# One layer of a hybrid decoder on one core: two-pass broadcasts and gates, longer pauses, two-block attention, and half of the score scaling on GpSimd

## The chip, the cores and the metric

One Trainium2 chip, one of its cores. The time is device microseconds of one launch of the whole layer. A core has TensorE (matrix products; the profile calls it PE, its weight loads PEld), VectorE (DVE), ScalarE (ACT), GpSimd (POOL) and SyncE (SP, which here issues nearly all DMAs). The profile's clock column is the share of TensorE's full clock that was granted.

## What is computed

One layer of a decoder, 1024 tokens of 1024 channels, in float32. Three token mixers run on the same normalised input and are merged:

```python
u = rmsnorm(h, norm_mix)
(aq, ak, av, az, aa, ab,  bq, bk, bv, bo, bi, bf,
 cq, ckc, cvc, cks, cvs, ckw, cvw, cg, mg) = split_cols(u @ w_in, IN_SIZES)
y_a = gated_deltanet(aq, ak, av, az, aa, ab, ...)   # 4 heads of 128, chunks of 64
y_b = mlstm(bq, bk, bv, bo, bi, bf, ...)            # 4 heads of 128, chunks of 64
y_c = nsa(cq, ckc, cvc, cks, cvs, ckw, cvw, cg, ...)  # 8 query heads, 2 key groups, width 64
br = einsum("bsnc,ncd->bsnd", stack([y_a, y_b, y_c]), w_branch)
h = h + (sum over branches of sigmoid(mg) * br) @ w_out
h = h + (silu(u1 @ w_gate) * (u1 @ w_up)) @ w_ffn_out          # u1 = rmsnorm(h), inner width 2816
h = h + sigmoid(u2 @ w_ple_gate) * (p @ w_ple_proj)            # u2 = rmsnorm(h)
```

The DeltaNet mixer solves a unit triangular system for each chunk (here in blocks of 16, then two levels of products) and runs a scan over the chunks. The mLSTM mixer has exponential gates with a running maximum and a scan. The third mixer adds three attentions for each query: over 63 compressed blocks, over four selected blocks of 64 keys, and over a window of 512 keys; each has its own softmax and its own gate (`cg`), and the compressed scores choose the selected blocks.

## The kernel before

**Two-part products.** Most large products are made of float32 values split in two parts of a shorter type (float32r): `hi` is a rounded copy that ScalarE makes, `lo` the rest, `x - hi`, that VectorE or GpSimd makes. A product is then three products, hi x hi, hi x lo and lo x hi (`chan_block`, `tok_block`). Each weight block is 128 x 2048 and comes as four DMAs into `wraw`; `halve` (L429, L431) splits it into `whi` and `wlo` one block ahead, `load` fetches two blocks ahead. In the third stage VectorE makes every second `wlo`, in the others GpSimd makes all of them. A few products are in full float32; each of them shows as two records in the trace.

**Three stages.** The first runs the input projection as a list of blocks: the projection of `p`, the gates block, then for each DeltaNet head two blocks (q, k and v, z) and two or three blocks of merge gates for the first half of the tokens, then eight mLSTM blocks, five attention blocks and two more gate blocks. The second runs ten blocks of merge gates for the other half of the tokens, with attention beside them. The third runs the last two gate blocks, the six branch projections, the output projection, the FFN (its first pair of blocks as plain products, the ten others by a seven-product scheme on combined inputs, `utT1` to `utT4`), and the last gate.

**Sides.** Beside the blocks run generators ("sides") that issue the small work: gates, solves, scans, mLSTM heads and attention. A block yields between its groups of products, and `advance(n)` then lets the sides take n steps. At each of these `woven` grows by 1.4, the time of the block's products in that step. `pause(us)` stops a side until `woven` has grown by so much, so that products of blocks are issued to TensorE ahead of what follows; `behind()` ties the next products behind the block's last product. `later(lag, f)` calls f when the blocks' own product time has passed the lag. The rate is 2 steps in the first stage and 3.8 in attention. Each engine runs its queue in order; the order within the program is set at build time by a planner with its own costs, following the order in which the program was written where nothing stands against it. Named tiles come from pools: ten half tiles (`b2`), eleven and six whole tiles, eight banks of the product memory; a tile whose buffers are all in use waits for one.

**What the change touches.**

- `gates_block` (L609): 40 gate columns times `u`, one output tile, 2 halves x 8 x 3 products, then a scaled copy into `gaterows`; `gates_side` (L626) transposes that with eight small products (`gtr`) and derives all gates.
- `row_bcast` (L741): spreads a column over all rows. GpSimd multiplies the identity by the column (L747, `gcb_d`, `mrb_d`), and a full float32 product with a matrix of ones gives `gcb` (DeltaNet) or `mrb` (mLSTM). Two halves per head, four heads each.
- `gdn_solve` (L798): decay matrices, convolutions (L786), norms (`ktr`, L838), Gram matrices, the 16-wide triangular inverse on VectorE (`zb`, `xb`) with two trips through memory, a pause of 14, then the products `levq`, `levv`, `levw`, `levx`, `levy`. `levq` needs `gW` (L908).
- `nsa_keys` (L1243): splits and transposes keys (`khht`, `khtr`), with a pause of 3 before each half's transposes.
- `nsa_attend` (L1348): the list of attention tasks, window (w) or selected (s), query tile 0 to 7, pair of heads hp 0 or 1. Each turn issues the scores of one task in four steps and, in between, the values of the task before. `att_query` (L1377) loads, scales, splits and transposes a query tile (`qstk`, `qtr`) when its first scores begin. `att_scores` (L1400): the products `S`, the sum with the bias and the maximum on VectorE (L1453 to L1466), the exponential on ScalarE (L1472), then for each group and pair of heads on VectorE:

```python
nc.vector.tensor_tensor(sm[:, g], sm[:, g], gate[:, g], OP.mult)
for i in (n - 1, n):
    nc.vector.tensor_scalar(pts[i][:, :nk], pts[i][:, :nk], sm[:, g, i % 2:i % 2 + 1], None, OP.mult)
```

  (L1476, L1478). `att_values` (L1554): for each block of 128 keys four transposes (`ptr`) into one bank, a copy to `PT` by ScalarE or VectorE, and, one block behind, two value products (`nso`); at the end the compressed values, two products on quarters of the array (`nso<-PT,cv`).
- `load_y` (L1612): loads and splits a branch's output, all eight tiles at once.
- `ffn_combine` (L1754): sums of parts of `u`, whose low parts GpSimd makes (L1764). `put` (L1793) splits an activation, its low part (`alo`, L1796) on GpSimd.
- `ple_blocks`: the last addition (L1967) on GpSimd, then the store.

Of the kernel before, what the change touches and what calls it, by code (L numbers as in the profile page):

```python
# [38 lines left out]
COMBINE_LAG = 8.0  # L39
CMP_AT = 1, 3  # L40
# [19 lines left out]
def _constants():  # L60
# [44 lines left out]
    add("rowscale", np.where((m >= 4) & (m < 8), -1.0, 1.0))  # L105
# [30 lines left out]
def _blocks(w_in, w_branch, w_out, w_ffn_in, w_ffn_out, w_ple_gate, w_ple_proj):  # L136
# [7 lines left out]
    for dst, src, n in ((0, 2048, 4), (4, 4108, 4), (8, 2052, 4), (12, 4104, 4), (16, 5392, 24)):  # L144
        rows[:, dst:dst + n] = w_in[:, src:src + n]
# [81 lines left out]
class Trunk:  # L227
# [381 lines left out]
    def gates_block(self):  # L609
# [4 lines left out]
        def evac(ct, hf, ps):  # L614
            if hf == 0:
                self.tc.keep_in_program_order(
                    nc.vector.tensor_tensor(bias, self.chan["rowb"], self.rowscale, OP.mult))
            nc.scalar.activation(rows[:40, hf * 512:hf * 512 + 512], ps[:40], AF.Identity,
                                 bias=bias[:40], scale=self.rowscale[:40])
            if hf == 1:  # L620
                self.flags.add("rows")

        self.gaterows = rows
        return self.chan_block(self.u, evac, ncols=1)

    def gates_side(self):  # L626
# [3 lines left out]
        ps = self.ps("gtr")  # L630
        for tt in range(NT):
            self.tr(ps[:, tt * 40:tt * 40 + 40], self.gaterows[:40, tt * P:tt * P + P])
        gm = self.b2("gm")[:, :320].rearrange("p (t c) -> p t c", c=40)
        nc.scalar.activation(gm, ps[:, :320].rearrange("p (t c) -> p t c", c=40), AF.Copy)
# [39 lines left out]
        self.cum, self.gcol = cum, gcol  # L674
# [62 lines left out]
        self.ms, self.msc, self.msi, self.memt, self.mwks, self.mr = s, sc, si, emt, wks, r  # L737
# [3 lines left out]
    def row_bcast(self, col, name):  # L741
# [3 lines left out]
        for hf in range(2):  # L745
            d = self.b2(name + "_d")
            nc.gpsimd.tensor_tensor(d[:, :].rearrange("p (t c) -> p t c", c=P), bc(self.ident.unsqueeze(1), [P, 4, P]),  # L747
                                    bc(col[:, 4 * hf:4 * hf + 4].unsqueeze(2), [P, 4, P]), OP.mult)
            ps = self.ps(name)
            self.mm(ps, self.ones, d)  # L750
            out.append(ps)
# [46 lines left out]
    def gdn_solve(self, h):  # L798
# [10 lines left out]
        dps = self.row_bcast(self.cum[:, :, h], "gcb")  # L809
# [20 lines left out]
        for w in H:  # L830
            for hf in H:
# [8 lines left out]
                yield from self.pause(1.4)  # L840
# [69 lines left out]
        yield from self.pause(14.0)  # L910
# [136 lines left out]
    def mls_side(self, h):  # L1047
# [6 lines left out]
        dps = self.row_bcast(self.mr[:, :, h], "mrb")  # L1054
# [188 lines left out]
    def nsa_keys(self, n, i):  # L1243
# [9 lines left out]
        for hf in range(2):  # L1253
# [10 lines left out]
            yield from self.pause(3.0)  # L1264
# [10 lines left out]
    def nsa_compress(self):  # L1275
# [3 lines left out]
        cv = self.small("cv", [P, 64])  # L1279
# [3 lines left out]
        for i, n in enumerate("kv"):  # L1283
# [13 lines left out]
            dst = ckr if n == "k" else cv  # L1297
# [9 lines left out]
            for g in range(2):  # L1307
                nc.vector.tensor_copy(dst[64 * g:64 * g + 63], ps[64 * g:64 * g + 63, :64])
# [28 lines left out]
        self.dump("cv", cv)  # L1337
# [10 lines left out]
    def nsa_attend(self):  # L1348
# [12 lines left out]
        for t in tasks + [None]:  # L1361
            a = self.att_scores(*t) if t else iter(())
# [698 lines left out]
```

## Time and profile before

| | |
|---|---|
| median of three runs | 2394.88 us (2393.13 to 2399.14) |
| the profiled execution: its time, its span | 2392.93 us, 2391.1 us |
| mean granted clock of TensorE | 0.987 |
| busy: TensorE, VectorE, ScalarE, GpSimd | 2286.2, 1338.2, 856.3, 782.9 us |
| first stage | 0 to about 918 us |
| attention | about 918 to 1311 us |
| branches, output projection | about 1311 to 1575 us |
| FFN, last gate | about 1575 to 2391 us |

A product's time in the profile is from its start to its modelled end, and the next one starts before that end. What a product costs TensorE is therefore read from one start to the next. "Busy" of TensorE counts any time with a product under way.

### The profile page before, as it was taken

To read this page: it belongs to the slowest core of one execution; us is meant where nothing else is said; L and a number is where in the kernel's file an instruction comes from. 1 tells how busy PE (TensorE), PEld (TensorE's weight loads), DVE (VectorE), ACT (ScalarE), POOL (GpSimd) and SP (SyncE) were. 2 spreads that over 40 slices of the span, in tenths; PEclk is the share of its full clock that TensorE was granted. 3 is DMA by queue.
4 is the path that set the end of the run, shared out by engine and by line. 5 is a ranking of instruction groups with operands and counts; after the bars stand their busy time and mean duration, and the time that the engine had idled before them with its cause. 6 is when DMAs were issued, how large, how long until landed. Compare 5 with 4: busy or idle time off the path is not lost.

```text
span 2391.1 us, 34586 instructions
## 1 busy us (share of the span) xinstructions
PE 2286.2 (96%) x12840; PEld 1829.4 (77%) x12840; DVE 1338.2 (56%) x3088; ACT 856.3 (36%) x1832; POOL 782.9 (33%) x662
## 2 busy tenths in 40 slices
PE   8989898989999998999999999998999999999999
PEld 6777677878778996666665778986777777777789
DVE  5455555643223436888775446677555555555583
ACT  6424242423222334545454322452222222222362
POOL 2342424322122123322121151235444444444434
PEclk9999999999999999999999999999999999999999
DMA  6131212121122123111111643311111111111143
GB/s 230 50 96 40 92 40 65 59 64 45 63 77 80 45 93 107 58 54 45 50 45 50 228 164 129 128 57 36 53 49 54 49 49 51 51 53 53 53 133 128
DMA packets 121887, 183.05 MB, mean 77 GB/s; under 512 B 25275, under 2 KB 47204, under 8 KB 121720
## 3 DMA queue, kind: packets, MB, share of 16 engines
q1 hardware_dynamic: 121432, 180.72, 22.5%
q8 instruction: 101, 1.65, 0.3%
q14 instruction: 66, 0.54, 0.1%
q10 hardware_dynamic: 288, 0.14, 0.0%
HBM read 149.04 MB, written 31.76 MB: 76 GB/s over the span
## 4 chain that ended last, share of the span: by engine, by line
PE 77%; DVE 12%; issue 4%; POOL 3%; DMA 3%; ACT 2%; SPq 0%; POOLq 0%; ACTq 0%; DVEq 0%
PE mm L242 60%; PE nso L242 3%; PE ptr L250 2%; PE S L242 2%; POOL wlo L431 2%; DVE P L1478 1%; DVE zb L893 1%; DVE xb L894 1%; PE mops L242 1%; PE gks L242 1%; PE gpu L242 1%; ACT g_junk L838 1%; POOL alo L1796 1%; ACT whi L429 1%; PE levq L242 1%
## 5 line engine op out<-in xcount | busy, mean ns | idle before, releaser
L431 POOL TENSOR_TENSOR wlo<-wraw,whi 128x512 fp32r<-128x512 f32 x334 | 449.7, 1351 | 1063.9 <-ACT whi L429 818.9
L242 PE MATMUL mm<-u,whi 128*128 128x512 f32 x1888 | 632.7, 410 | 2.0 <-ACT mg L1606 2.0
L429 ACT ACTIVATE whi<-wraw 128x512 fp32r<-128x512 f32 x408 | 255.7, 630 | 470.2 <-PE mm L242 384.0
L242 PEld LDWEIGHTS mm<-u,whi 128*128 128x128 f32 x1888 | 341.4, 190 | 76.0 <-issue 11.5
L242 PE MATMUL mm<-u,wlo 128*128 128x512 f32 x944 | 379.2, 402 | 0.0
L242 PEld LDWEIGHTS mm<-u,wlo 128*128 128x128 f32 x944 | 178.3, 189 | 39.4 <-issue 1.2
L1839 DVE TENSOR_TENSOR fc<-fc,mm 128x512 f32<-128x512 f32 x140 | 95.3, 686 | 159.0 <-PE mm L242 158.9
L1880 DVE TENSOR_TENSOR h<-h,mm 128x512 f32<-128x512 f32 x176 | 118.6, 684 | 74.6 <-PE mm L242 72.1
L242 PE MATMUL mm<-whi,alo 128*128 128x512 f32 x352 | 141.6, 402 | 6.8 <-POOL alo L1796 6.8
L242 PE MATMUL mm<-whi,ahi 128*128 128x512 f32 x352 | 140.7, 400 | 5.5 <-ACT whi L429 5.5
L242 PE MATMUL mm<-wlo,ahi 128*128 128x512 f32 x352 | 140.6, 399 | 2.5 <-POOL wlo L431 2.5
L431 POOL TENSOR_TENSOR wlo<-ws,whi 128x512 fp32r<-128x512 f32 x60 | 84.3, 1405 | 148.7 <-ACT whi L429 148.7
L242 PE MATMUL mm<-u2hi,whi 128*128 128x512 f32 x304 | 121.1, 398 | 0.0
L242 PE MATMUL mm<-u2lo,whi 128*128 128x512 f32 x304 | 121.1, 398 | 0.0
L242 PE MATMUL mm<-u2hi,wlo 128*128 128x512 f32 x304 | 120.3, 396 | 0.0
L1472 ACT ACTIVATE P<-P,n_ng 128x640 f32<-128x640 f32 (+7 forms) x128 | 93.0, 728 | 64.1 <-DVE n_ng L1470 61.1
L429 ACT ACTIVATE whi<-ws 128x512 fp32r<-128x512 f32 x60 | 37.8, 630 | 174.9 <-DVE h L1880 130.4
L250 PE MATMUL ptr<-ident,P 128*128 128x128 f32 x528 | 89.8, 282 | 7.3 <-DVE P L1478 5.5
L250 PEld LDWEIGHTS ptr<-ident,P 128*128 128x128 f32 x528 | 59.6, 140 | 47.2 <-issue 28.3
L242 PE MATMUL mm<-whi,u 128*128 128x256 f32 x512 | 94.1, 283 | 0.1
L431 DVE TENSOR_TENSOR wlo<-wraw,whi 128x512 fp32r<-128x512 f32 x74 | 69.5, 939 | 35.5 <-ACT whi L429 35.4
L242 PEld LDWEIGHTS mm<-whi,alo 128*128 128x128 f32 x352 | 66.8, 190 | 27.2 <-POOL alo L1796 11.6
(497 smaller groups left out, 5048.9 us busy)
## 6 DMA issues: line engine op xcount, KB each, us to landing
wraw<-in_w_dram SPq DMA_DIRECT2D x408, 256.0 KB, 2.7
mgs<-mg SPq DMA_DIRECT2D x48, 256.0 KB, 2.3
mgld<-mgs SPq DMA_DIRECT2D x48, 256.0 KB, 5.6
xt<-in_x_dram SPq DMA_DIRECT2D x8, 512.0 KB, 4.8
xt<-in_x_dram SPq DMA_DIRECT2D x32, 128.0 KB, 3.7
sg<-pps SPq DMA_DIRECT2D x32, 128.0 KB, 3.5
out_dram<-sg SPq DMA_DIRECT2D x32, 128.0 KB, 2.8
pps<-ppst SPq DMA_DIRECT2D x8, 256.0 KB, 2.0
```

Source lines behind the costliest of these rows:

```text
L242: return self.nc.tensor.matmul(out, lhsT, rhs, start=start, stop=stop).ins
L250: self.nc.tensor.transpose(out, in_, self.ident[:n, :n])
L429: nc.scalar.activation(hi, t, AF.Copy)
L431: eng.tensor_tensor(lo, t, hi.bitcast(F32), OP.subtract)
L838: nc.scalar.activation(junk, ps[:, q * P:q * P + P], AF.Square, accum_out=ssq[:, w, 4 * hf + q:4 * hf + q + 1])
L893: nc.vector.tensor_tensor(tmp[:, :m, m:], bc(Z[:, :m, m:m + 1], shp), bc(X[:, m:m + 1, m:], shp), OP.mult)
L894: nc.vector.tensor_tensor(X[:, :m, m:], X[:, :m, m:], tmp[:, :m, m:], OP.subtract)
L1472: nc.scalar.activation(pts[i][:, :nk], pts[i][:, :nk], AF.Exp, bias=ng[:, i:i + 1], accum_out=sm[:, g, i % 2:i % 2 + 1])
L1478: nc.vector.tensor_scalar(pts[i][:, :nk], pts[i][:, :nk], sm[:, g, i % 2:i % 2 + 1], None, OP.mult)
L1796: nc.gpsimd.tensor_tensor(lo, t, hi.bitcast(F32), OP.subtract)
L1839: nc.vector.tensor_tensor(t, x, ps, OP.add)
L1880: nc.vector.tensor_tensor(self.h[tt][s], self.h[tt][s], ps, OP.add)
```

## The change

- **Gates in two passes.** The 40 gate columns are put a second time at columns 64 to 103 of the block, and four copies on VectorE replace their high parts by the low parts (`k2`). Products with the 128 columns give the high rows at 0 to 39 and the low rows at 64 to 103 at once, so that two products (with `u` high and `u` low) replace three; the low x low term comes with them. `gates_side` transposes both groups of rows and adds them.
- **Broadcasts in two passes.** The column is split in a high and a low column (`col_split`); two diagonal tiles and two float32r products with ones, added in the same bank, replace one float32 product.
- **Pauses:** 14 to 24 in the solve; 1.4 to 3.0 behind the query transposes of its norms; 3 to 6 for the first half in `nsa_keys`.
- **Attention.** `att_query` is called one task ahead, its transposes at that task's fourth step; `att_values` takes two blocks a step, transposes of a pair first, then the value products of the pair before; values start after the second step of the scores; the compressed values have `cv` laid out with zeros for the other group, so that one product of 128 x 128 replaces two of 64 x 64; the gate is the second scalar of the scaling, and of each pair the first head is scaled on GpSimd.
- **Low parts.** `load_y` delays the splits of the second and third branch; in `ffn_combine`, in `put` for the first two tiles and for the first half of each odd tile, and in the last addition, VectorE takes GpSimd's place.

The diff, cut to its core:

```diff
@@ _blocks
-        rows[:, dst:dst + n] = w_in[:, src:src + n]
+        rows[:, dst:dst + n] = rows[:, 64 + dst:64 + dst + n] = w_in[:, src:src + n]
@@ gates_block
+        def gen(wb):
+            for wh, wl in wb:
+                k2 = lambda t: t[:, :].rearrange("p (k c) -> p k c", k=2)[:, :, 64:104]
+                nc.vector.tensor_copy(k2(wh), k2(wl).bitcast(F32))
+            for hf in range(2):
+                ps = self.ps("mm", "mm")
+                for kc in range(KC):
+                    uh, ul = self.u(kc, hf)
+                    w = wb[kc // 2][0][:, kc % 2 * 256:kc % 2 * 256 + P]
+                    self.mm(ps, w, uh, kc == 0, False)
+                    self.last_mm = self.mm(ps, w, ul, False, kc == KC - 1)
...
@@ gates_side
+        for r in (0, 64):
...
+                self.nc.tensor.transpose(ps[:, tt * 40:tt * 40 + 40], self.gaterows[r:r + 40, tt * P:tt * P + P],
+                                         self.ident[r:r + 40, r:r + 40])
...
+                nc.vector.tensor_tensor(gm, gm, p3, OP.add)
@@ row_bcast
-            self.mm(ps, self.ones, d)
+            for i, col in enumerate(cols):
+                d = self.b2(name + "_d", F32R)
+                nc.gpsimd.tensor_tensor(...)
+                self.mm(ps, self.ones_r, d, i == 0, i == 1)
@@ gdn_solve
-                yield from self.pause(1.4)
+                yield from self.pause(3.0 if w else 1.4)
...
-        yield from self.pause(14.0)
+        yield from self.pause(24.0)
@@ nsa_keys
-            yield from self.pause(3.0)
+            yield from self.pause(6.0 if hf == 0 else 3.0)
@@ nsa_attend
-            nb = prev["nb"] + 2 if prev else 0
+            nb = -(-prev["nb"] // 2) + 2 if prev else 0
...
-                upto = -(-nb * (i + 1) // 4)
+                upto = -(-nb * i // 3)
...
+                if after and after[0] == "w" and after[2] == 0:
+                    if i == 0:
+                        ahead = self.att_query(after[1])
+                        next(ahead)
+                    elif i == 3:
+                        next(ahead)
@@ att_scores
-                nc.vector.tensor_tensor(sm[:, g], sm[:, g], gate[:, g], OP.mult)
                 for i in (n - 1, n):
-                    nc.vector.tensor_scalar(pts[i][:, :nk], pts[i][:, :nk], sm[:, g, i % 2:i % 2 + 1], None, OP.mult)
+                    (nc.vector if i % 2 else nc.gpsimd).tensor_scalar(
+                        pts[i][:, :nk], pts[i][:, :nk], sm[:, g, i % 2:i % 2 + 1], gate[:, g, i % 2:i % 2 + 1],
+                        OP.mult, OP.mult)
@@ att_values
-        for kb in range(nb + 1):
+        pend = []
+        for kb in range(0, nb + 2, 2):
+            new = []
+            for b in range(kb, min(kb + 2, nb)):
...
-            for g in range(2):
-                gp = slice(64 * g, 64 * g + 64)
-                self.mm(o[gp, cols], st["cv"][gp], ct[gp, :256], False, hp == 1)
+            self.mm(o[:, cols], st["cv"].rearrange("p g d -> p (g d)"), ct[:, :256], False, hp == 1)
@@ load_y
+                    self.later(Y_LAG + 2.56 * (4 * hf + kk), lambda kk=kk, hf=hf, t=t: parts(kk, hf, t))
@@ ffn_combine, put, ple_blocks
-            nc.gpsimd.tensor_tensor(lo, t, hi.bitcast(F32), OP.subtract)
+            nc.vector.tensor_tensor(lo, t, hi.bitcast(F32), OP.subtract)
...
-            nc.gpsimd.tensor_tensor(lo, t, hi.bitcast(F32), OP.subtract)
+            (nc.vector if f < 2 or f % 2 and hf == 0 else nc.gpsimd).tensor_tensor(lo, t, hi.bitcast(F32), OP.subtract)
...
-                nc.gpsimd.tensor_tensor(t, t, h, OP.add)
+                nc.vector.tensor_tensor(t, t, h, OP.add)
```

More of the change, by code (lines that the diff above doesn't have):

```diff
@@ L39 @@
 COMBINE_LAG = 8.0
+Y_LAG = 9.0
 CMP_AT = 1, 3
@@ L104, in _constants @@
     add("sent", np.broadcast_to(np.array([-1e6, -2e6, -3e6, -4e6]), (P, 4)))
-    add("rowscale", np.where((m >= 4) & (m < 8), -1.0, 1.0))
+    add("rowscale", np.where((m % 64 >= 4) & (m % 64 < 8), -1.0, 1.0))
     def onehot(dist, shift):
@@ L629, in gates_side @@
         yield from self.need("rows")
-        ps = self.ps("gtr")
-        for tt in range(NT):
-            self.tr(ps[:, tt * 40:tt * 40 + 40], self.gaterows[:40, tt * P:tt * P + P])
         gm = self.b2("gm")[:, :320].rearrange("p (t c) -> p t c", c=40)
-        nc.scalar.activation(gm, ps[:, :320].rearrange("p (t c) -> p t c", c=40), AF.Copy)
+        for r in (0, 64):
+            ps = self.ps("gtr")
+            for tt in range(NT):
+                self.nc.tensor.transpose(ps[:, tt * 40:tt * 40 + 40], self.gaterows[r:r + 40, tt * P:tt * P + P],
+                                         self.ident[r:r + 40, r:r + 40])
+            p3 = ps[:, :320].rearrange("p (t c) -> p t c", c=40)
+            if r == 0:
+                nc.scalar.activation(gm, p3, AF.Copy)
+            else:
+                nc.vector.tensor_tensor(gm, gm, p3, OP.add)
         yield
@@ L807, in gdn_solve @@
         half = lambda ap, hf: ap[:, hf * 512:hf * 512 + 512]
-        dps = self.row_bcast(self.cum[:, :, h], "gcb")
+        dps = self.row_bcast([c[:, :, h] for c in self.cumhl], "gcb")
         yield
@@ L1360, in nsa_attend @@
         prev = None
-        for t in tasks + [None]:
+        for _ in self.att_query(0):
+            pass
+        for n, t in enumerate(tasks + [None]):
             a = self.att_scores(*t) if t else iter(())
+            after = (tasks + [None] * 2)[n + 1]
             b = self.att_values(prev) if prev else iter(())
             cur = None
-            nb = prev["nb"] + 2 if prev else 0
+            nb = -(-prev["nb"] // 2) + 2 if prev else 0
             done = 0
@@ L1397, in att_query @@
             out.append(t)
-        return out
+        yield
     def att_scores(self, br, qt, hp):
@@ L1572, in att_values @@
                     nc.scalar.activation(pt, ps, AF.Copy)
-            if pend is not None:
-                b, pt_ = pend
+                new.append((b, pt))
+            for b, pt_ in pend:
                 for g in range(2):
@@ L1614, in load_y, with parts @@
         res = {}
+        def parts(kk, hf, t):
+            hi, lo = self.l2("yhi", F32R), self.l2("ylo", F32R)
+            self.split(hi, lo, t, scale)
+            res[kk, hf] = (hi, lo)
         for hf in range(2):
```

58 lines of the change are left out of this document (34 added, 24 removed).

## The prediction

> **What bounds the kernel now.** I read the page first, its busy times and the chain that ended last.
>
> ```profile
> span 2391.1 us, 34586 instructions
> ...
> PE 2286.2 (96%) x12840; PEld 1829.4 (77%) x12840; DVE 1338.2 (56%) x3088; ACT 856.3 (36%) x1832; POOL 782.9 (33%) x662
> ...
> PE 77%; DVE 12%; issue 4%; POOL 3%; DMA 3%; ACT 2%; SPq 0%; POOLq 0%; ACTq 0%; DVEq 0%
> ```
>
> TensorE is busy for 96% of the span and carries 77% of the chain; no other engine is near its limit over the whole span. So the time falls only where TensorE has fewer slots to run, or where it now waits. Second came the view of waits, for TensorE alone. Its columns: engine, tile waited with, releaser, total us, times, longest.
>
> ```profile
> PE levq L242 <- DVE gW L908: 30.0, 4, 8.5
> PE mm L242 <- POOL alo L1796: 6.8, 11, 1.7
> PE mm L242 <- POOL wlo L431: 6.2, 7, 2.5
> PE qtr L248 <- DVE qstk L1388: 6.2, 8, 1.7
> PE mm L242 <- ACT whi L429: 5.5, 1, 5.5
> PE ptr L250 <- DVE P L1478: 5.5, 12, 0.8
> ...
> PE khtr L248 <- ACT khht L1261: 3.2, 2, 1.7
> PE ktr L250 <- ACT g_junk L838: 3.0, 3, 1.3
> PE nso L242 <- DVE PT L1570: 3.0, 3, 1.5
> ```
>
> One wait stands out: four times, once per DeltaNet head, TensorE sits up to 8.5 us until VectorE's block-inverse is ready. The rest are many small ones. Third came the view by stages: the 10 us behind each of these four waits, the attention stage, and the entrance to the FFN in two pieces. Behind the stretch and its length stand the busy times of TensorE, weight load, VectorE, ScalarE, GpSimd, then the granted clock.
>
> ```profile
> 159.70:169.70 10.00, 10.00 (x154) 8.00 (x156) 2.67 (x4) 0.92 (x2) 2.54 (x2) 0.77 0.09 28
> 278.60:288.60 10.00, 9.97 (x144) 8.00 (x146) 2.67 (x4) 0.63 (x1) 2.54 (x2) 0.74 0.08 28
> 396.50:406.50 10.00, 10.00 (x172) 8.18 (x173) 2.67 (x4) 0.00 (x0) 1.05 (x1) 0.83 0.01 2
> 503.00:513.00 10.00, 10.00 (x140) 8.22 (x140) 2.67 (x4) 0.00 (x0) 1.05 (x1) 0.69 0.01 2
> ...
> 918.00:1311.00 393.00, 372.77 (x2144) 243.97 (x2144) 311.13 (x1146) 200.74 (x448) 93.29 (x91) 1.00 0.15 52
> 1589.00:1631.40 42.40, 35.20 (x151) 27.79 (x149) 40.03 (x38) 16.00 (x29) 28.70 (x19) 0.97 0.07 25
> 1631.40:1641.40 10.00, 7.48 (x22) 5.61 (x23) 7.26 (x9) 3.35 (x6) 10.00 (x7) 0.62 0.23 79
> ```
>
> A long wait costs twice: after it TensorE is full (10.00 of 10) but at 0.69 to 0.83 of its clock. In attention VectorE is the second engine, 311 of 393 us; GpSimd has room, 93.
>
> **The change, part by part.** The profiled execution took 2392.9 us (span 2391.1), 2.0 below the median of the three runs, 2394.9; the sum is made against 2392.9 and 2 is added at the end.
>
> *Pacing.* The solve's pause goes from 14 to 24. A pause ends on whole steps of 1.4, so it lasts 18 steps instead of 10: 8 x 1.4 = 11.2 us more of projection blocks are issued to TensorE ahead of the level products. That is more than the longest wait, 8.5, so all 30.0 us are filled with work that would otherwise come later. What goes with the wait is the slow clock behind it: 10 us times (1 - 0.77), (1 - 0.74), (1 - 0.83) and (1 - 0.69) make 2.3 + 2.6 + 1.7 + 3.1 = 9.7. Together 39.7. The two small pauses add at least one step (1.4) before the waits `ktr` (longest 1.3) and two steps before `khtr` (longest 1.7): 3.0 + 3.2 = 6.2 gone. Pushed back with the solve is its scan, which then runs while VectorE does the next head's convolutions; scan steps go back and forth between TensorE and VectorE and queue behind them. Nothing here shows that price; between 0 and half of the 39.7 I take 4, nearer to nothing, since a head's scan already runs beside the blocks without a row of its own among the large waits.
>
> *Two-pass broadcasts.* One pair of broadcasts, and the slot of a plain product:
>
> ```profile
> 177.05 1.88 PE L242 MATMUL gcb<-gcb_d,c 128*128 128x512 f32 x4
> 178.37 1.02 PE L242 MATMUL mm<-u,whi 128*128 128x512 f32 x2
> 179.23 0.40 PE L242 MATMUL mm<-u,wlo 128*128 128x512 f32 x1
> 179.46 0.38 PE L242 MATMUL gks<-gS,kT 128*128 128x128 f32 x2
> ```
>
> Ends overlap, so I count from start to start. A plain two-part-type product takes 179.46 - 179.23 = 0.23. The pair of full-precision products appears as four records and takes 178.37 - 177.05 = 1.32; the two products behind it take 0.86 where two slots are 0.46, so 0.40 more: 1.72. The new pair is four products of 0.23, 0.92. Saved 0.8 a pair, eight pairs (four heads of two mixers): 6.4. GpSimd makes twice as many diagonal tiles, 16 more; at about 1.1 us (the two-input tile priced below) that is 18 us more on an engine 33% busy, ahead of the use. I take nothing for them.
>
> *Two-pass gates.* The block drops from 48 products to 32: 16 x 0.23 = 3.7. Added are eight transposes:
>
> ```profile
> 65.14 0.44 PE L250 MATMUL gtr<-ident,gaterows 40*128 40x40 f32 x4
> 65.50 0.73 PE L242 MATMUL mm<-u,whi 128*128 128x512 f32 x2
> ```
>
> Four take 0.36, eight 0.7: net 3.0. The four copies of low weight parts into the high tiles sit on VectorE before the block's first product; the weights are split during the block before, so they have cover; without it, at most some 1 us, once.
>
> *Attention on TensorE.* One alternating stretch and one where two groups of value products stand together:
>
> ```profile
> 1112.92 0.65 PE L242 MATMUL nso<-PT,nvw 128*64 128x256 f32 x4
> 1113.50 0.66 PE L250 MATMUL ptr<-ident,P 128*128 128x128 f32 x4
> 1114.09 0.65 PE L242 MATMUL nso<-PT,nvw 128*64 128x256 f32 x4
> ...
> 1118.56 1.08 PE L242 MATMUL nso<-PT,nvw 128*64 128x256 f32 x8 [1.25 <-DVE PT L1570]
> 1119.57 0.66 PE L250 MATMUL ptr<-ident,P 128*128 128x128 f32 x4
> ```
>
> A group alone takes 0.58, two together 1.01, so a merge saves 0.15; merged transposes (0.59 each here) save between nothing and the same. By the loops there are 132 blocks, and two at a time leave 76 steps: 56 merges, 8.4 us, up to 17 with the transposes. Scores get placed between groups, so I take 6. The compressed-value product becomes one full-width product in place of two quarter ones; no such shape is in the trace; between 0 and 16 x 0.58 / 2 = 4.6 I take 0, since the two quarters may already run side by side. The waits: the query is prepared one task ahead (`qtr`, 6.2), values start one scoring step later (`ptr`, 5.5), value products trail by two blocks (`nso`, 3.0): 14.7. But value steps fall from 132 + 32 to 76 + 32 at an unchanged rate of 3.8 steps per 1.4 us of gate products, so the stage ends its own work earlier and is denser before that; I take half, 7. The query load moves up on SP's queue past weight loads and gets its buffer earlier; if no buffer were free those loads would queue behind it, covered by a block's lead. Attention: 13.
>
> *One head on GpSimd.*
>
> ```profile
> L1478 DVE TENSOR_SCALAR P<-P,n_sum 128x640 f32<-128x640 f32 (+7 forms) x128 | 70.5, 591 | 0.8
> ...
> L1476 DVE TENSOR_TENSOR n_sum<-n_sum,cgate 128x2 f32<-128x2 f32 x64 | 19.4, 304 | 0.7
> ```
>
> VectorE loses all of L1476, 19.4, and half of L1478, 35: 311 falls to 257. How the two engines get on:
>
> ```profile
> 1060.43 1.01 DVE L1478 TENSOR_SCALAR P<-P,n_sum 128x640 f32<-128x640 f32 x2
> ...
> 1068.23 2.31 DVE L1478 TENSOR_SCALAR P<-P,n_sum 128x640 f32<-128x640 f32 x2
> ```
>
> ```profile
> 1067.91 2.28 POOL L1422 TENSOR_TENSOR nearm<-near,n_msk 128x512 f32<-128x512 f32 x2
> ```
>
> The same two scalings take 1.01 alone and 2.31 while GpSimd works. No GpSimd scaling is in the trace: between VectorE's 0.5 a tile and GpSimd's two-input 1.14 on 512, 1.4 on 640, I take 1.0, midway. 64 of them bring GpSimd from 93 to about 157 of 393. The weight splits queued behind one come at most 1.4 later. VectorE's relief is no term of the sum: TensorE sets the stage.
>
> [...]
>
> *FFN.* The steady wait on `alo` (6.8 over 11, one of them the entrance's 1.7) is 0.5 at each pair of blocks; the late half goes to VectorE:
>
> ```profile
> 1592.32 0.68 DVE L1776 TENSOR_TENSOR uw<-uw 128x512 f32<-128x512 f32 x1
> ...
> 1594.66 1.78 DVE L1769 TENSOR_TENSOR uw<-u2hi,u2lo 128x512 f32<-128x512 f32 x1
> ```
>
> ```profile
> 1594.15 1.74 POOL L1764 TENSOR_TENSOR utT3l<-uw,utT3h 128x512 fp32r<-128x512 f32 x1
> ```
>
> 0.68 instead of 1.74 is 1.1 sooner, twice the wait: 5 gone. At the entrance VectorE is busy 40.0 of 42.4 us, and it gets 20 more subtractions (16 of the combinations, 4 of the first activations), 13.6. But its own take 1.78 beside GpSimd and 0.68 alone, so clearing GpSimd gives back about as much and more. Of the waits there (5.5, 2.5, 1.7) I take 5, the ends being nothing and all with the 0.62 clock behind them, 12.
>
> *Deferred splits of the branch outputs, final add on VectorE:* off the waits above; nothing.
>
> Sum: 39.7 + 6.2 - 4 + 6.4 + 3.0 + 13 + 5 + 5 = 74.3; 2392.9 - 74.3 = 2318.6, and with 2 for the median about **2320 us**.
>
> **The rivals.** *The pacing wait comes back.* The chain behind the solve is fixed in time; if scans and convolutions collide on VectorE, half of the 39.7 returns at scan steps or the next `ktr`: plus 20, 2340. For: the scan is a chain of short steps. Against: TensorE has 11.2 us of work for a wait of 8.5.
> [...]
> *Slower: every pair waits for its GpSimd half.* At GpSimd's slow rate (1.74 on 512, so 2.2 on 640), behind VectorE's 0.5, a pair is ready after 2.7 instead of 1.01: 1.7 x 64 = 109 in attention, where nothing is gained: 2320 + 13 + 109 = 2442. It decides from 61 / 64 = 0.96 us uncovered per pair. Against: in the profile before, TensorE waited for `P` only 12 times, and the change lets values start later.
> *The pauses do nothing,* because the planner orders the queues by its own costs: plus 46, 2366. Against: the products are tied behind the last block product.
> *Better:* the other half of attention's waits, the merged transposes, all of the entrance, no new wait: 7 + 11 + 7 + 4 = 29, 2291.
>
> **How the numbers follow.** Forecast (about 2307 to 2328) 0.45; better 0.18; lock 0.13; pacing back 0.12; both of these, 2353, 0.05; pauses without effect 0.02; the slow rival 0.05, of which 0.02 about its crossing point. The range 2290 to 2352 leaves out the last three. 0.3% is 7 us, about what the three runs (2393.1 to 2399.1) can tell. Faster 0.95, same 0.02, slower 0.03.
>
> **What would show it.** Right: the `levq <- gW` row gone and full clock from 150 to 515 us; broadcasts as four records within about 0.9 us; no `qtr <- qstk`; the 0.5 waits on `alo` gone; attention from 393 to about 380 us. Wrong: new rows for `gpv`, `gpu` or `ktr` of several us; waits on `P` with GpSimd as releaser; attention as long as before with VectorE still above 300 us; a wait of 5 us or more at the FFN's entrance.

## The result, and the profile after

The changed kernel took 2329.18 us, median of four runs (2327.68 to 2333.68), against 2394.01 for the kernel before: ratio 0.9728, 95% interval 0.9709 to 0.9748. Forecast were 2320, a range of 2290 to 2352, and faster with 0.95. The gain is 64.8 us, where the sum had 74.3. The profiled execution is the longest of the four, 2333.68 us; the other three lie between 2327.7 and 2329.4. Of all runs below one execution was slow (2625.05 us, of the kernel with `gV` on VectorE), and the ratios leave it out.

From the page of the kernel after: the span, the busy times and the chain.

```profile
span 2331.9 us, 34557 instructions
...
PE 2262.2 (97%) x12800; PEld 1836.5 (79%) x12800; DVE 1304.0 (56%) x3032; ACT 850.4 (36%) x1832; POOL 792.9 (34%) x680
...
PE 42%; DVE 3%; ACT 1%; DMA 1%; issue 0%; POOL 0%; SPq 0%; ACTq 0%; POOLq 0%; DVEq 0%
```

TensorE is still the bound. (The chain's shares add up to less than half of the span, so I don't lean on it.) TensorE's largest waits in the kernel after, with total us, times and longest:

```profile
PE ptr L251 <- POOL P L1526: 16.8, 22, 1.3
...
PE gytr L251 <- DVE vtok L1050: 5.4, 2, 3.1
...
PE mm L243 <- POOL wlo L432: 4.7, 5, 3.7
...
PE mtr L251 <- DVE m_tmp L737: 2.9, 1, 2.9
```

The 30.0 of `levq` are gone, and `qtr`, `ktr`, `nso` and `alo` with them. Four rows are new or larger: a wait for GpSimd's half of the scaled scores, the DeltaNet output transposes, one long wait for a weight's low part, and one in the gates' chain (2.9, where before 1.1 stood). Of the prediction's signs of being wrong one is among them: waits for `P` with GpSimd as the releaser. Now the stretch from 150 to 515 us, which holds the four old `levq` waits, in the kernel before and after (stretch, length, busy times of TensorE, weight load, VectorE, ScalarE, GpSimd, granted clock):

```profile
150.00:515.00 365.00, 331.65 (x2253) 268.08 (x2252) 203.34 (x402) 113.96 (x296) 121.92 (x109) 0.95 0.20 62
```

```profile
150.00:515.00 365.00, 352.85 (x2321) 285.70 (x2321) 197.28 (x412) 114.78 (x304) 132.73 (x119) 0.99 0.21 65
```

More busy time at a better clock, but neither is full. Behind four of the new waits (`mtr`, `wlo`, and `gytr` twice) stands a slow clock again:

```profile
74.50:84.50 10.00, 9.92 (x32) 7.97 (x33) 6.70 (x23) 2.44 (x7) 4.58 (x4) 0.68 0.01 2
...
164.80:174.80 10.00, 9.95 (x63) 7.89 (x64) 0.50 (x1) 1.19 (x2) 1.25 (x1) 0.83 0.25 80
233.00:243.00 10.00, 9.90 (x42) 8.11 (x43) 5.95 (x19) 2.07 (x9) 0.83 (x2) 0.83 0.21 80
346.00:356.00 10.00, 9.16 (x39) 7.86 (x40) 7.03 (x20) 2.67 (x10) 2.16 (x3) 0.83 0.24 93
```

To see where the time went, I cut the span at two marks that every kernel has: the first transposes of the attention queries (`qtr`) and the first of the normalised FFN input (`u2tr`). The rows that give them, before and then after (first and last start follow the durations):

```profile
L248 PE MATMUL qtr<-ident_r,qstk x64: 222/250/279, 920.1 to 1205.3; 128*128 128x128 f32 x64
L250 PE MATMUL u2tr<-ident,xn x128: 270/272/330, 1516.6 to 2312.9; 128*128 128x128 f32 x128
```

```profile
L249 PE MATMUL qtr<-ident_r,qstk x64: 223/249/413, 889.5 to 1145.5; 128*128 128x128 f32 x64
L251 PE MATMUL u2tr<-ident,xn x128: 270/272/328, 1476.7 to 2255.3; 128*128 128x128 f32 x128
```

The same cut for every kernel that was run (profiled executions, us; the ratio is to the kernel before, from all runs):

| kernel | ratio, 95% interval | first stage | attention, branches | FFN, last gate |
|---|---|---|---|---|
| before | 1 | 920.1 | 596.5 | 874.5 |
| after | 0.9728 (0.9709 to 0.9748) | 889.5 | 587.2 | 855.2 |
| before, longer pauses alone | 0.9883 (0.9870 to 0.9897) | 894.8 | 596.8 | 873.9 |
| after, all scaling on VectorE | 0.9714 (0.9701 to 0.9728) | 885.1 | 582.1 | 855.2 |
| after, one-pass broadcasts | 0.9755 (0.9742 to 0.9769) | 892.3 | 588.1 | 855.3 |
| after, low parts on GpSimd | 0.9825 (0.9811 to 0.9838) | 890.8 | 590.9 | 873.3 |
| after, `gV` on VectorE | 0.9713 (0.9700 to 0.9727) | 884.2 | 590.6 | 853.5 |
| after, later scan output | 0.9711 (0.9698 to 0.9725) | 879.6 | 590.0 | 854.5 |
| after, `alo` on GpSimd | 0.9769 (0.9756 to 0.9783) | 889.5 | 590.3 | 859.9 |
| after, one block a step | 0.9805 (0.9791 to 0.9818) | 886.8 | 603.0 | 854.4 |
| after, three repairs | 0.9662 (0.9647 to 0.9677) | 872.7 | 585.2 | 852.1 |
| after, four repairs | 0.9651 (0.9637 to 0.9665) | 869.3 | 582.5 | 854.5 |
| after, entrance on GpSimd | 0.9775 (0.9759 to 0.9791) | 886.4 | 587.0 | 862.7 |
| after, gates as before | 0.9755 (0.9739 to 0.9772) | 890.7 | 589.7 | 855.2 |

Six of these have the first stage of the kernel after unchanged, and it took 885.1 to 890.8 in them (mean 888.0): a stage is good to some 3 us. Much of that spread is the clock behind the four new waits. They stand in all six kernels with nearly the same lengths, but the 10 us behind each lose a different amount to the slow clock: 8.2 to 8.5 us in all where the stage took 889.5 to 890.8, 4.8 and 4.9 where it took 886.4 and 886.8, and 3.4 where it took 885.1. By these means the first stage gained 32 us, the middle 7 (589.2 over eight kernels with after's attention), the FFN with the last gate 20 (854.4 over nine with after's). The sum had 51.3, 13 and 10. (These add to 59, the difference of the two profiled executions; by the medians it is 64.8.)

### The profile page after: what moved, and what is told of

Its sections match the earlier page's. It is cut to its first block, busy times and chain, and to the rows that moved or that the text cites. A ratio compares the mean times of both kernels' runs of the same rounds, so it can differ in the third digit from the quotient of the medians.

```text
span 2331.9 us, 34557 instructions
## 1 busy us (share of the span) xinstructions
PE 2262.2 (97%) x12800; PEld 1836.5 (79%) x12800; DVE 1304.0 (56%) x3032; ACT 850.4 (36%) x1832; POOL 792.9 (34%) x680
## 5 line engine op out<-in xcount | busy, mean ns | idle before, releaser
L432 POOL TENSOR_TENSOR wlo<-wraw,whi 128x512 fp32r<-128x512 f32 x334 | 443.1, 1333 | 938.5 <-ACT whi L430 740.1
L243 PE MATMUL mm<-u,whi 128*128 128x512 f32 x1888 | 625.5, 408 | 3.3 <-ACT mg L1656 2.1
L243 PE MATMUL mm<-u,wlo 128*128 128x512 f32 x928 | 373.9, 403 | 3.7 <-POOL wlo L432 3.7
L1526 POOL TENSOR_SCALAR P<-P,n_sum,cgate 128x640 f32<-128x640 f32 (+7 forms) x64 | 66.1, 1033 | 156.6 <-DVE n_sum L1523 99.7
L251 PE MATMUL ptr<-ident,P 128*128 128x128 f32 x528 | 82.7, 280 | 17.4 <-POOL P L1526 16.8
```

The costliest lines, as they stand in the source:

```text
L243: return self.nc.tensor.matmul(out, lhsT, rhs, start=start, stop=stop).ins
L251: self.nc.tensor.transpose(out, in_, self.ident[:n, :n])
L432: eng.tensor_tensor(lo, t, hi.bitcast(F32), OP.subtract)
L1526: (nc.vector if i % 2 else nc.gpsimd).tensor_scalar(pts[i][:, :nk], pts[i][:, :nk], sm[:, g, i % 2:i % 2 + 1], gate[:, g, i % 2:i % 2 + 1] ...
```

## The experiments

**The longer pauses alone**, put into the kernel before:

```diff
-        yield from self.pause(14.0)
+        yield from self.pause(24.0)
...
-                yield from self.pause(1.4)
+                yield from self.pause(3.0 if w else 1.4)
...
-            yield from self.pause(3.0)
+            yield from self.pause(6.0 if hf == 0 else 3.0)
```

> The kernel before with the three longer pauses alone. Theory A: the pauses remove the four waits on gW with their slow clock (39.7 us) and the small waits on ktr and khtr (6.2), and what eats the first stage's gain in the changed kernel (30.6 us there instead of 51 forecast) is the doubled GpSimd work of the broadcasts; then the pauses alone are worth 40 to 44 us, about 2352. Rival B: the pauses push each scan into the next head's convolutions, and the waits on gytr, gpu and gks (8 us and some slow clock) come with the pauses alone; then they are worth about 30 us, about 2364.

Measured: 2367.26, ratio 0.9883, 28 us, the smaller of the two sizes expected. In the waits of this kernel `levq` is gone, and these stand there:

```profile
PE mm L242 <- POOL wlo L431: 10.1, 8, 4.0
...
PE gytr L250 <- DVE vtok L1012: 5.4, 2, 3.1
...
PE gks L242 <- DVE gS L994: 2.4, 1, 2.4
PE gpu L242 <- DVE gvn L987: 2.2, 2, 1.2
```

So the shortfall comes with the pauses themselves, not with the change's other parts: two of the new waits of the kernel after are already here, with nearly the same lengths (3.1 for `gytr`, 4.0 for `wlo`, which is 3.7 there).

**All scaling on VectorE:**

```diff
-                    (nc.vector if i % 2 else nc.gpsimd).tensor_scalar(
+                    nc.vector.tensor_scalar(
```

> The changed kernel with all 128 score scalings on VectorE, the gate still the second scalar. Theory A: the 16.8 us of waits for the GpSimd half in 22 places go, VectorE does the pair in about 1.0 us, attention is 8 to 14 us shorter, about 2318. Rival B: the relief of VectorE is needed; with 35 us more there the transposes wait for VectorE as they did before, and the time is the same or up to 5 us longer, 2329 to 2334.

Measured: 2327.68, ratio 0.9714. Against the kernel after the ratios differ by 0.14%, less than their intervals, but the middle part is shorter by 5.1 us here and by some 6 in all three runs with this edit (582.1, 585.2, 582.5 against a mean of 589.2). The split to GpSimd costs time, though less than the 8 to 14 us of theory A. The attention's stretch, in the kernel after and in this one:

```profile
887.00:1274.00 387.00, 365.28 (x2114) 257.10 (x2114) 267.77 (x1018) 200.06 (x448) 157.19 (x155) 1.00 0.16 53
```

```profile
882.60:1264.60 382.00, 368.00 (x2118) 257.82 (x2119) 296.56 (x1082) 201.69 (x448) 93.03 (x91) 1.00 0.16 54
```

The split does take 29 us off VectorE and put 64 on GpSimd, and TensorE's idle time is 21.7 with it and 14.0 without. One step of the kernel after, in which VectorE starts first, and one in which GpSimd does, show why:

```profile
1024.19 0.61 DVE L1526 TENSOR_SCALAR P<-P,n_sum,cgate 128x640 f32<-128x640 f32 x1
...
1024.34 1.22 POOL L1526 TENSOR_SCALAR P<-P,n_sum,cgate 128x640 f32<-128x640 f32 x1 [2.74 <-DVE n_sum L1523]
...
1025.61 0.66 PE L251 MATMUL ptr<-ident,P 128*128 128x128 f32 x4 [0.75 <-POOL P L1526]
```

```profile
1100.33 0.87 POOL L1526 TENSOR_SCALAR P<-P,n_sum,cgate 128x640 f32<-128x640 f32 x1 [5.76 <-DVE n_sum L1523]
1100.37 1.18 DVE L1526 TENSOR_SCALAR P<-P,n_sum,cgate 128x640 f32<-128x640 f32 x1
```

The two hold each other up. In these two steps the one that starts first takes 0.61 on VectorE or 0.87 on GpSimd; the one behind it takes longer, 1.22 or 1.18. Two more pairs fit: started 0.07 and 0.20 behind GpSimd's scaling, VectorE's took 1.15 and 1.02, so each ended 1.22 after GpSimd's start. The pair is ready when the slow one is, 1.37 after the start in the first step (1025.56 - 1024.19) and 1.22 in the second; without the hold the first would take an estimated 1.02 (0.15 + 0.87). In this experiment VectorE does both in 1.14:

```profile
1015.97 1.14 DVE L1526 TENSOR_SCALAR P<-P,n_sum,cgate 128x640 f32<-128x640 f32 x2
```

and it can, with 296.56 of 382 us busy.

**One-pass broadcasts:**

```diff
-        self.cumhl, self.gcol = self.col_split("cum", cum[:, :, 0:4]), gcol
...
+        self.cumhl, self.gcol = (cum[:, :, 0:4],), gcol
...
-                d = self.b2(name + "_d", F32R)
+                d = self.b2(name + "_d")
...
-                self.mm(ps, self.ones_r, d, i == 0, i == 1)
+                self.mm(ps, self.ones, d)
```

> The changed kernel with the broadcasts as one float32 product and one GpSimd tile again. Theory A: the second GpSimd tiles beside the gates' chain on VectorE cause the 2.9 us wait before the first broadcast and the 6.8 us of half clock behind it (3.4 lost); without them about 6 come back while the broadcasts cost TensorE 6.4 more: 2327 to 2331, no difference. Rival B: the extra tiles are hidden; 6.4 slower, about 2336.

Measured: 2337.46, ratio 0.9755, 6.5 us above the kernel after (0.0027 x 2394), with intervals that overlap. The size agrees with the 6.4 forecast and with rival B. Of the 2.9 that `mtr` waits in the gates' chain 1.1 is left, as in the kernel before, so 1.8 of it belong to the two-pass broadcasts, as theory A had it; but `gks` with 2.4 and `gpu` with 2.2 are back, as in the run with the pauses alone.

**Low parts back on GpSimd,** all three of the change's (the FFN's input, `alo`, the last addition):

```diff
-            nc.vector.tensor_tensor(lo, t, hi.bitcast(F32), OP.subtract)
+            nc.gpsimd.tensor_tensor(lo, t, hi.bitcast(F32), OP.subtract)
...
-            (nc.vector if f < 2 or f % 2 and hf == 0 else nc.gpsimd).tensor_tensor(lo, t, hi.bitcast(F32), OP.subtract)
+            nc.gpsimd.tensor_tensor(lo, t, hi.bitcast(F32), OP.subtract)
...
-                nc.vector.tensor_tensor(t, t, h, OP.add)
+                nc.gpsimd.tensor_tensor(t, t, h, OP.add)
```

> The changed kernel with the low parts of the FFN and the last addition on GpSimd as before; the delayed splits of the branch outputs stay. Theory A: the FFN's 19.4 us of gain is these moves: the waits at the entrance (7.6), their slow clock (some 2) and ten waits of 0.5 on alo come back, 12 to 18 us slower, about 2344. Rival B: VectorE was full at the entrance anyway and the gain there came from the order of the work; less than 6 us slower, below 2335.

Measured: 2353.77, ratio 0.9825: 23 us above the kernel after by the ratios, 19 above the mean in the FFN's part, more than twice the 10 of the prediction. Two runs below ask which of the three carries it.

**`gV` on VectorE.** In the kernel after GpSimd's queue at the one long `wlo` wait reads:

```profile
162.09 1.04 POOL L946 TENSOR_TENSOR gV<-zd,c 128x512 f32<-128x512 f32 x1 [6.48 <-DMA zd<-xds]
163.09 2.96 POOL L432 TENSOR_TENSOR wlo<-wraw,whi 128x512 fp32r<-128x512 f32 x2
```

```diff
-        for eng, M, w in ((nc.gpsimd, V, 0), (nc.vector, W, 1)):
+        for eng, M, w in ((nc.vector, V, 0), (nc.vector, W, 1)):
```

> The kernel after, with gV made on VectorE beside gW instead of on GpSimd; nothing else. In the kernel after GpSimd sat idle for 6.48 us until 162.09 us for the zd transfer that gV needs, and the next block's wlo stood behind gV: TensorE waited 3.70 us for wlo at 164.85 us and then ran 3.4 us at half clock. Theory A (in-order queue of GpSimd): wlo no longer stands behind the transfer, the wait and its half clock go, and the kernel is 4 to 6 us faster than after (ratio to before about 0.970, against 0.9728). Theory B (the wait only moves): VectorE now does two products behind the same transfer, the scan steps and the first level product come later by some 0.8 us, new waits of levq, gks or gytr take the place, and the time is within 2 us of after.

Measured: 2326.56, ratio 0.9713, 3.6 us under the kernel after, within the intervals. The wait is gone from the rows: `wlo` from GpSimd has 1.0 in four places, the longest 0.3, and GpSimd has all four low parts by 157.59 us, before the transfer lands for which `gV` on VectorE waits until 163.29:

```profile
152.07 5.52 POOL L432 TENSOR_TENSOR wlo<-wraw,whi 128x512 fp32r<-128x512 f32 x4 [4.68 <-ACT whi L430]
```

The first stage is 3.8 us under the mean of 888.0. So the place and the mechanism are shown; the size is just under theory A's 4 to 6, at the edge of what can be told.

**A later scan output:**

```diff
-        yield from self.pause(8.0)
+        yield from self.pause(14.0)
         yT = self.a4("gyT")
```

> The kernel after, with the pause ahead of the scan's output transposes (gytr) at 14 instead of 8; nothing else. In the kernel after gytr waited 5.4 us in two places (3.09 us at 233.1 us), each followed by a 3.4 us stretch at half clock, because the small rsqrt steps on VectorE that it needs took 1.13 to 1.19 us each beside wlo on GpSimd (0.17 us without). Theory A (the pause is only too short): the waits and the two half-clock stretches go, 5.4 + 3.4 = 8.8 us at most, and the kernel is 4 to 9 us faster than after. Theory B (the output displaced further collides with the next head's convolutions, as the pauses alone did): the waits come back at gks, gpu or the next head's ktr, and the time is within 2 us of after or above it.

Measured: 2325.83, ratio 0.9711, 4.1 us under the kernel after; the first stage is 8.4 under the mean. No `gytr` row is left and nothing new stands in its place. Theory A.

**`alo` alone on GpSimd,** the second edit of the three:

> The kernel after, with the low parts of the FFN's hidden values (alo, the line of put) all on GpSimd as before; the low parts of the FFN's input and the last addition stay on VectorE. With all three on GpSimd the time was about 23 us above after, where the prediction had 5 for alo and 5 for the entrance. Theory A (alo is the dear part: GpSimd is nearly full in the FFN, and alo's delays pass on to wlo): most of the 23 us is here, 14 to 22 us above after, with waits of alo, wlo and whi of more than 15 us together. Theory B (the entrance is the dear part, by its 13.7 us of half clock): 5 to 8 us above after.

Measured: 2339.95, ratio 0.9769: 9.8 above the kernel after by the ratios, 5.5 above the mean in the FFN's part. Its waits there are:

```profile
PE mm L243 <- POOL alo L1855: 5.2, 10, 0.5
...
PE mm L243 <- DVE sil L1864: 2.0, 1, 2.0
```

That is the steady 0.5 at each pair of blocks that the prediction read in the kernel before, and in that part it costs about what it shows. (The 2.0 for `sil` stands where the kernel after waits 2.1 for `utT4h`.) The time lies between the two theories, nearer to B: `alo` is the smaller part of the 23.

**The entrance alone on GpSimd,** the first edit of the three:

> The kernel after, with the low parts of the FFN's input (the line of part) on GpSimd as before; alo and the last addition stay on VectorE. All three on GpSimd cost some 23 us, alo alone 10.3 by the ratios. Theory A (the entrance is the second dear part, by its waits and the half clock after them): 8 to 13 us above after, with a half-clock stretch of more than 10 us near 1590 us. Theory B (the last addition on GpSimd is what made up the rest, since wlo of the last gate's blocks stands behind it): 2 to 6 us above after, as the prediction's 5 for the entrance.

Measured: 2337.68, ratio 0.9775, 11.3 above the kernel after by the ratios, 8.3 above the mean in the FFN's part: theory A. (The 10.3 that it has for `alo` is 9.8 by the ratios.) The waits and the clock of this kernel there:

```profile
1586.30 0.80 PE L243 MATMUL mm<-whi,ahi 128*128 128x512 f32 x1 [6.11 <-ACT whi L430]
1589.70 0.79 PE L243 MATMUL mm<-wlo,ahi 128*128 128x512 f32 x1 [2.61 <-POOL wlo L432]
```

```profile
1577.00:1640.00 63.00, 53.55 (x220) 42.13 (x219) 41.52 (x50) 18.69 (x32) 32.07 (x23) 0.92 0.13 44
```

In the kernel after the same place has 2.1 us idle in 60 and a clock of 0.97:

```profile
1580.00:1640.00 60.00, 57.92 (x242) 46.29 (x242) 37.62 (x52) 17.97 (x30) 23.86 (x19) 0.97 0.16 53
```

5.5 and 8.3 leave some 5 of the 18.9 in the FFN's part for the last addition and for what the parts do to each other; the addition alone was not run.

**One block a step,** as before, with the scores' four steps filled as before:

```diff
-            nb = -(-prev["nb"] // 2) + 2 if prev else 0
+            nb = prev["nb"] + 2 if prev else 0
...
-                upto = -(-nb * i // 3)
+                upto = -(-nb * (i + 1) // 4)
...
-        for kb in range(0, nb + 2, 2):
+        for kb in range(0, nb + 1):
             new = []
-            for b in range(kb, min(kb + 2, nb)):
+            for b in range(kb, min(kb + 1, nb)):
```

> The kernel after, with the attention's values done one key block at a time and spread over the scores' four steps as before; the queries one step ahead, the scaling on two engines and the joined compressed product stay. Theory A (the prediction's 6 us for merging): TensorE goes from transposes to products twice as often, and the attention stage is 5 to 7 us longer, about 2335 on the scale of after's 2329. Theory B (merging is worth nothing beside the wait for GpSimd's scaling): within 2 us of after. Theory C (two blocks ask for the scaled rows sooner, so that merging pays for itself with the 16.8 us of waits for GpSimd): one block at a time is faster than after by 2 us or more.

Measured: 2347.18, ratio 0.9805: 18.4 above the kernel after by the ratios, 13.8 above the mean in the middle part. Theory A has the sign, at less than half the size. The run undoes the later start of the values too (`upto`), so it prices both together. This kernel's attention, to be held against the 365.28 of 387 above:

```profile
885.00:1290.00 405.00, 377.75 (x2129) 251.58 (x2130) 280.38 (x1018) 200.38 (x447) 157.30 (x154) 1.00 0.15 51
```

12.5 us more busy time of TensorE and 5.5 more idle. Two blocks a step save mostly TensorE's own time; that it is saved at the turns between transposes and value products is the prediction's reading, and no run separates them.

**Three repairs together** (all scaling and `gV` on VectorE, the later scan output):

> The kernel after with three of the runs' findings put together: all of the attention's scalings on VectorE, gV on VectorE, and the pause ahead of gytr at 14. Alone they lay 3, 3.6 and 4 us under after by their ratios. Theory A (three separate places, the first in the attention, the others in two different heads): the gains add up, 9 to 11 us under after, a ratio to before of 0.968 to 0.969, with the waits of gytr and of the 3.7 us wlo gone and ptr's for GpSimd replaced by 7.5 us for VectorE. Theory B (the steps pass on to each other, because each one moves what VectorE does next): less than 6 us under after, ratio 0.9705 or more.

Measured: 2310.85, ratio 0.9662, 15.8 under the kernel after; the single gains add up to 11.1 (3.4, 3.6, 4.1), and the intervals don't separate the two. Theory A: the gains add up, if anything to more than the 9 to 11 expected.

**Four repairs.** The fourth aims at the wait in the gates' chain. Its place in the kernel after, with GpSimd's diagonal tiles of the new broadcasts:

```profile
72.08 1.04 POOL L785 TENSOR_TENSOR gcb_d<-ident,cumhi 128x512 fp32r<-128x512 f32 x1
73.07 0.18 DVE L706 TENSOR_TENSOR ekd<-ekd,beta 128x32 f32<-128x32 f32 x1
73.08 1.08 POOL L785 TENSOR_TENSOR gcb_d<-ident,cumlo 128x512 fp32r<-128x512 f32 x1
73.18 1.26 DVE L721 TENSOR_TENSOR_SCAN m_crow<-m_srow 32x128 f32<-32x128 f32 x1
...
74.58 0.28 PE L251 MATMUL mtr<-ident,m_crow 32*128 32x32 f32 x1 [2.89 <-DVE m_tmp L737]
```

Beside these tiles the scan takes 1.26 us, and a step before it (`negc`) 0.77; in the kernel before, with one-pass broadcasts, the same two took 0.41 and 0.18, without such a tile beside them.

```diff
-        yield from self.pause(2.0)
+        yield from self.pause(6.0)
         ps = self.ps("mtr2")
```

> The run with three repairs, and the pause in the gates' chain ahead of the second mtr at 6 instead of 2. In the kernel after mtr waits 2.89 us at 74.58 us, because four gcb_d of 1.04 us follow one another on GpSimd just there and VectorE's scan before it starts at 73.18, when the third of them ends; 6.8 us at half clock follow. Theory A (mtr comes too soon): the wait and its half clock go, up to 2.9 + 3.4 = 6.3 us faster than with three repairs. Theory B (the gates' chain is what the first head's solve waits for, in one order on the side): everything of the first head comes some 4 us later, other waits appear, and the time is within 2 us of the run with three.

Measured: 2308.64, ratio 0.9651, 2.6 us under the three repairs by the ratios, which their intervals don't separate; the first stage is 3.4 shorter. The `mtr` wait is gone. (The 6.3 counted on 6.8 us at half clock behind it; in the run with three repairs it was half of that, a clock of 0.83 in the 10 us behind.) This version is the fastest of all: 3.5% under the kernel before, 0.8% under the change. Its clock in the stretch where the kernels before and after had 0.95 and 0.99, and in the one where the kernel after had 0.68:

```profile
150.00:515.00 365.00, 361.89 (x2469) 294.35 (x2468) 203.67 (x419) 120.36 (x318) 140.53 (x127) 1.00 0.22 66
```

```profile
74.50:84.50 10.00, 10.00 (x45) 8.14 (x45) 7.08 (x21) 3.50 (x9) 4.56 (x4) 1.00 0.01 2
```

**The gates as before:** the three products of `chan_block` for the 40 columns, one group of transposes, no addition.

> The kernel after, with the gates as before: three products of each chunk and half instead of two, no copy of the low columns into the high tile, one transposition instead of two and no addition. Theory A (the prediction's 3.0 us): 2 to 4 us above after. Theory B (the first stage fell short by what the new gates add: eight more transposes, an addition on VectorE ahead of the gates' chain, and the chain's meeting with the four gcb_d): the time is after's or up to 4 us below it, and mtr's wait of 2.89 us changes.

Measured: 2335.20, ratio 0.9755, 6.5 above the kernel after; the first stage is 2.7 above the mean. Theory A by sign; the size can't be told from the forecast's 3.0. `mtr` waits 2.9 here too, so the new gates are not its cause.

## Why the prediction was right, and where it was not

**Right: the bound, the sign, the range.** TensorE is the bound, and most of what was to be taken from it or from its waits came off the time. The sum was 9.5 us too large (15 on profiled executions): two of its parts were too large, by 19 and 6 us, and one too small by 10. That the errors partly cancel is luck.

**Pacing: the failed step.** "Between 0 and half of the 39.7 I take 4, nearer to nothing, since a head's scan already runs beside the blocks without a row of its own." The pauses' terms came to 41.9 (39.7 + 6.2 - 4), and the pauses alone shortened the first stage by 25.3. The `levq` waits went as read; of the small pauses' 6.2, `ktr`'s 3.0 went and 1.5 of `khtr`'s 3.2 stayed. But the row that was missing in the kernel before said nothing about a scan that runs 11 us later: there it met other work. The prediction's rival of a returning wait, plus 20, had the size, not the place. It looked at the scan's own steps and at `ktr`. What came was: the scan's output step, whose small VectorE steps lie beside GpSimd's weight splits (5.4); and a weight split queued on GpSimd behind `gV`, which waits for a transfer (3.7). The wait in the gates' chain grew from 1.1 to 2.9 by the broadcasts' doubled tiles. Of the prediction's own test, "the `levq` row gone and full clock from 150 to 515 us", the first half was right and the second wrong (0.99). The repairs bear out the three causes together: with these waits taken away, the first stage takes 869.3, so 50.8 us less than before, where the forecast had 51.3 for it. These waits are 12.0 us (5.4, 3.7, 2.9); the slow clock behind them is 3.2 + 1.7 + 1.7 + 1.7 = 8.3 in the four windows shown, and 6.4 in the mean of the six kernels whose mean stage is 888.0. Together 18.4, and the repairs brought 18.7 (888.0 - 869.3). One by one the repairs show less: they shortened the stage by 8.4, 3.8 and 3.4, where a stage is good to some 3.

**Broadcasts: right.** The new four products in the kernel after, by the prediction's own count from start to start:

```profile
188.82 1.18 PE L243 MATMUL gcb<-gcb_d,ones_r 128*128 128x512 f32 x4
189.83 0.62 PE L243 MATMUL mm<-u,whi 128*128 128x512 f32 x2
190.29 0.39 PE L243 MATMUL mm<-u,wlo 128*128 128x512 f32 x1
```

1.01 for the four, and the two products behind take their plain 0.46; 1.72 before. Saved 0.71 a pair, 5.7 in all, where 6.4 was forecast. "I take nothing" for GpSimd's 16 more tiles was wrong at one place at least: the first head's four stand in the way of the gates' chain.

**Gates: 3.0 agrees with what was measured** (2.7 in the first stage, 6.5 by the ratios), and no run pins it closer.

**Attention: 13 forecast, 7 measured, from three sizes that were off.** Merging was "8.4, up to 17 with the transposes … I take 6": the upper end was nearer (13.8 to 18.4, with the later start of the values). The waits of 14.7, of which half were to go, went as rows, but 16.8 for GpSimd's `P` took their place, so that idle time is 21.7 against 20.2 before. "VectorE's relief is no term of the sum: TensorE sets the stage" was right, and a price stood where no term stood: the split costs about 6. Without it the middle takes 583.3 (mean of three), 13.2 under before, the forecast number. The cause is in the trace: in the two steps shown, the later of two scalings is held up (GpSimd's takes 1.22 instead of 0.87, VectorE's 1.18 instead of 0.61). That ate 6 us, not all of attention's 13, with which the time would have been 2333. TensorE's waits have the form of the slow rival, a pair that waits for its GpSimd half, in 22 places with 0.76 each, not at all 64 with 1.7 (and 61 / 64, where that rival would have decided, is 0.95). The 1.0 taken for a GpSimd scaling lies between the 0.87 and the 1.22 of these steps; the 20 of 640 columns in the kernel after took 0.87 to 1.74. That "the two quarters may already run side by side", the reason for taking 0 for the joined compressed product, was an assumption that no trace shows: in the kernel before a pair of quarters takes 0.58 from start to start (1042.11 to 1042.69), in the kernel after the joined one 0.25 (1009.79 to 1010.04; 0.24 to 0.54 in all 16), and no run prices it alone.

**FFN: 10 forecast, 20 measured.** `alo` was about right: 5 forecast, 5.5 in that part. The entrance was the mis-sized term: 5 was taken between nothing and 12, and it measured 8.3 to 11.3, since most of the 0.62 clock behind the waits went too (over the 60 us from 1580 the clock was 0.91 before and 0.97 after). The remaining 6 or so were put at nothing ("final add on VectorE: off the waits above"); no run shows where in that part they are.

## What to carry to other kernels

When a wait is filled by moving work later, follow the moved work to its new place and list what each engine has queued there; a clean row at the old place is no evidence for the new one. Before putting half of a pair on a second engine, look whether the two engines hold each other up, and compare when the pair is complete, not how busy the first engine is: 1.37 against 1.14 us lost some 6 us in the attention although VectorE gained 29. A wait of 2 to 4 us of TensorE is worth counting one to two times: the clock behind it cost nothing, 1.7 or some 3.2 us here, for the same wait in different runs. A difference of 3 us between two profiles can be that alone. Look at what is queued behind an instruction that waits for a transfer: GpSimd's `gV` started 6.48 us late for one here, the next block's `wlo` behind it, and TensorE waited 3.7 us for that; with `gV` on VectorE no wait for GpSimd's `wlo` was over 0.3.

## What the runs showed of the hardware

**Short VectorE steps took longer beside long GpSimd steps: 1.13 to 1.19 us instead of 0.17.** Two rows of VectorE and one of GpSimd in the kernel after, in the chain ahead of `gytr`:

```profile
229.67 1.13 DVE L297 SCALAR_TENSOR_TENSOR rsq_tgo<-rsq_tgo,g_s 128x8 f32<-128x8 f32 x1
230.83 1.19 DVE L298 SCALAR_TENSOR_TENSOR rsq_ygo<-rsq_tgo,rsq_ygo 128x8 f32<-128x8 f32 x1
232.06 0.17 DVE L1045 TENSOR_TENSOR rsq_ygo<-rsq_ygo,g_rq 128x8 f32<-128x8 f32 x1
```

```profile
229.47 2.53 POOL L432 TENSOR_TENSOR wlo<-wraw,whi 128x512 fp32r<-128x512 f32 x2 [0.26 <-ACT whi L430]
```

A step on 8 columns takes 0.17 here, and 1.13 to 1.19 while GpSimd has one of two subtractions of 1.27 each under way; the last slow one ends at 232.02, with the second subtraction (232.00). The scalings of the attention, with one tensor and two scalars as inputs, hold each other up too, and in both directions: in the two steps shown, 0.87 on GpSimd and 0.61 on VectorE for the one that starts first, 1.22 and 1.18 for the one behind.

**Behind waits of 2 to 3 us stood a slow clock, and behind some of the same waits in other kernels a full one.** In the kernel after TensorE waits 2.08 us, and the next 10 us have a clock of 0.83:

```profile
1589.56 0.77 PE L243 MATMUL mm<-whi,ahi 128*128 128x512 f32 x1 [2.08 <-ACT utT4h L1821]
```

```profile
1588.00:1598.00 10.00, 8.45 (x30) 6.83 (x31) 9.81 (x17) 1.67 (x3) 0.00 (x0) 0.83 0.08 26
```

In steps of 0.4 us the clock granted here reads 0.50 from 1589.6 to 1592.8 and 1.00 from 1593.2 on; behind the 2.89 us wait it reads 0.50 from 74.4 to 80.8 and 1.00 from 81.2 on. At half clock, 0.17 of 10 us lost is a stretch of 3.4 us; the 0.68 behind the 2.89 us wait is one of 6.4 us.

The same waits in other kernels: `mtr` again 2.9 us, with all scaling on VectorE, and the first `gytr` again 3.1 us, with the entrance on GpSimd.

```profile
74.50:84.50 10.00, 9.98 (x44) 8.12 (x45) 6.98 (x21) 2.34 (x7) 4.69 (x4) 1.00 0.01 2
```

```profile
233.00:243.00 10.00, 9.81 (x48) 8.07 (x49) 6.39 (x20) 2.70 (x10) 2.04 (x3) 1.00 0.29 107
```

Where the kernel after had 0.68 and 0.83, the clock is full. What decides it no run here shows.
